# An encoder block: turned rows in another tile, the row blocks in another order

## The chip, the cores and the metric

The kernel runs on one core of one Trainium2 chip. A core has five engines that run side by side: TensorE (PE in the profile) multiplies matrices, VectorE (DVE) and ScalarE (ACT) work on rows of elements, GpSimd (POOL) does so too, and SyncE (SP) issues transfers. Each engine takes its instructions in the order of the program; semaphores make one wait for another. The metric is the device time of one execution in microseconds; smaller is better. Times in the text are microseconds from the start of the span unless said otherwise.

## The reference

One layer of a hybrid encoder on 1024 tokens (a grid of 16 rows and 64 columns) with 1024 channels, all in float32.

```python
u = rms_norm(x, norm1_g)
proj = u @ w_in
q, k, v, cb, cc, ch, ga, gb = split(proj)        # 512 x 6, then 1024 x 2
q, k = rms_norm(q per head, q_norm_g), rms_norm(k per head, k_norm_g)
y_a = neighbourhood_attention(q, k, v, rpb) @ w_attn_branch
y_b = (cb * conv3(cc * ch)) @ w_conv_branch
m = sigmoid(ga) * y_a + sigmoid(gb) * y_b
x = x + m @ w_o
x = x + relu(rms_norm(x, norm2_g) @ w_mlp_in)**2 @ w_mlp_out
```

The attention has 8 heads of 64 channels; each token looks at a window of 8 rows and 16 columns of the grid. The gates ga and gb are the projections that matter below as "the gates".

## The kernel before

**Arithmetic.** A float32 matrix is split into a high and a low half, both float16, after scaling by a power of two; a product is then three passes on TensorE (high by high, high by low, low by high; `PASSES`, L453). The high half is a scaled copy (ScalarE), the low half is the scaled value minus the high half (VectorE). The scale of a weight matrix needs a bound over all of it: squares with an accumulated sum on ScalarE (L266), a short sum on VectorE (L270, L272), a matmul with a matrix of ones, one column wide, that sums over the partitions (L201), and a few one-column instructions on VectorE. Only then are the high (L306) and low halves (L297) made.

**Rows.** The 1024 tokens are eight row blocks of 128. Row block b is loaded into `xt[:, b]` (L366). `norm` (L436) is a generator with four steps: the sum of squares (ScalarE, L439), the reciprocal root on GpSimd (L420, L421), the high half (L445, or GpSimd at L443 for blocks listed in `BYPOOL`), the low half (VectorE, L447). `ln_step(b, n)` runs n of these steps. The halves lie in `u16`, which has four places, block b in place b % 4. `turn_row(b)` (L518) has SyncE issue a transposing DMA of both halves into the columns of block b in `UT` (`uT` in the profile), from which TensorE reads them.

**V first, in two ways.** While the other blocks are still on their way, V of row blocks 0 and 1 is formed in float32 without the norm: `native_turn` (L563) transposes the raw rows on TensorE and stores them, scaled by the norm's gain, as `xT`; `native` (L574) multiplies them with V's raw weights, in two halves of 256 columns; `v_post` (L584) applies the row's scale and splits the result into `VT` (`vT`), which holds V as eight blocks of 128 tokens with a high and a low half. Before the change `xT` is a float32 view of the columns of row blocks 0 and 1 in `UT`, so that the two blocks are turned last. The other six blocks are V units, `v_unit` (L522): 24 matmuls of float16 halves and a split of the result into `VT[:, b]`.

**Q and K.** Sixteen units of 24 matmuls follow, eight row blocks for Q and eight for K (L743), each with a norm over each head (`qk_vec`). Weights come through a pool of five raw tiles; `load_upto(n)` issues loads up to tile n as the places come free. Tiles 0 to 3 are V's, 4 to 7 Q's, then K's. The preparation of a weight matrix (`prep`, L255) is a generator in `bg`, advanced by `tick`; work on the vector engines is in `fg`, advanced by `step`. What a unit leaves to be done with its result is put into `late` and done after the next unit's matmuls are in the queue, or at `settle()`.

**The gates' sums.** The gates use a scheme with seven instead of eight products, for which sums of row blocks n and n + 4 are formed from the normed rows: `sforms` (L481) scales both rows in place (ScalarE, L489), makes four sums in place (GpSimd, L493), and splits the pair into halves (L498, L500) that are stored to DRAM. `SFORM` (L479) lists the steps as (number of units done, n, whether it is the split).

The order of all this is written out by hand (L607 to L694). TensorE's queue holds: the transposes and float32 products with small sums between them, V units 2 to 7, then Q. SyncE's queue holds the loads and the transposing DMAs in the order written.

Of the kernel before, what the change touches and what calls it, by code (L numbers as in the profile page):

```python
# [10 lines left out]
F32 = mybir.dt.float32  # L11
# [4 lines left out]
OP = mybir.AluOpType  # L16
# [36 lines left out]
def encoder_block(ctx: ExitStack, tc: tile.TileContext, x, weights, cols, gqk, rel, masks, out):  # L53
# [12 lines left out]
    def bank(tag):  # L66
        return psum.tile([128, 512], F32, name="ps_" + tag, tag=tag, bufs=banks[tag])
# [29 lines left out]
    def at(c, i, n=1):  # L97
        return slice(c.start + i, c.start + i + n)
# [138 lines left out]
    def load_upto(n):  # L237
        while loaded[0] < min(n - held[0], limit[0], len(loads)):
            ch, p = loads[loaded[0]]
            loaded[0] += 1  # L240
            t = rawp.tile([128, 1024], F32, name="raw")
            load_into(t[:, :ch.widths[p][0] * ch.widths[p][1]], ch, p)
            ch.raw.append(t)
# [121 lines left out]
    def load_x(b):  # L365
        SP.dma_start(xt[:, b], x[b * 128:(b + 1) * 128, :])  # L366
# [10 lines left out]
    load_x(1)  # L377
    load_x(2)
    load_upto(4)
    load_x(3)  # L380
    load_x(4)
    SP.dma_start(gq.rearrange("p a d -> p (a d)"), bass.AP(tensor=gqk.tensor, offset=gqk.offset,
                                                           ap=[[0, 128], [1, 2 * HD]]))
    idi = w1p.tile([128, 128], I32, name="idi", bufs=1)
# [51 lines left out]
    def norm(xin, sq, u, y, pool):  # L436

        ss = tmp()
        A.activation(sq, xin, AF.Square, accum_out=sc[:, ss])  # L439
        yield  # L440
        yield from rpow(ss, D, y, 9)
        if pool:
            G.tensor_scalar(u[:, 0], xin, sc[:, y], 1.0, op0=OP.mult, op1=OP.mult)  # L443
        else:
            A.activation(u[:, 0], xin, AF.Copy, scale=sc[:, y])  # L445
        yield
        V.scalar_tensor_tensor(u[:, 1], xin, sc[:, y], u[:, 0], op0=OP.mult, op1=OP.subtract)  # L447

    def ln_turn(u16, b, dst):
        SP.dma_start_transpose(dst[:, :, :, b * 128:(b + 1) * 128].rearrange("p s k t -> p (s k) t"),  # L450
                               u16.rearrange("p s k -> p (s k)"))
# [19 lines left out]
    sgq, isgq = keep(), keep()  # L471
    sq = w1p.tile([128, D], F32, name="sq", bufs=1)
    ys = keep(8)
    BYPOOL = ()
    ln = [norm(xt[:, b], sq, u16[:, b % 4], at(ys, b), b in BYPOOL) for b in range(8)]
    GS = dram.tile([128, 4, 4, 2, 512], F16, name="gs")

    turned, formed = set(), [0]
    SFORM = ((7, 2, 0), (7, 3, 0), (8, 0, 0), (9, 1, 0), (9, 2, 1), (10, 3, 1), (11, 0, 1), (12, 1, 1))  # L479

    def sforms():  # L481

        for mark, n, split in SFORM:
            yield from apart(mark, 0)
            pair = xt[:, n:n + 5:4]
            if not split:
                assert n in turned and n + 4 in turned
                for b in (n, n + 4):
                    A.activation(xt[:, b], xt[:, b], AF.Copy, scale=sc[:, at(ys, b)])  # L489
                z = [xt[:, b, c:c + 512] for b in (n, n + 4) for c in (0, 512)]  # L490
                for o, a, b, op in ((3, 2, 3, OP.subtract), (2, 0, 2, OP.subtract),
                                    (0, 3, 0, OP.subtract), (1, 1, 0, OP.add)):
                    G.tensor_tensor(z[o], z[a], z[b], op=op)  # L493
                continue
            v = wqk.tile([128, 4, 2, 512], F16, name="s16", bufs=3)
            v4 = v.rearrange("p (b h) w c -> p b h w c", b=2)
            f = pair.rearrange("p b (h c) -> p b h c", h=2)
            A.activation(v4[:, :, :, 0], f, AF.Copy)  # L498
            yield
            V.tensor_tensor(v4[:, :, :, 1], f, v4[:, :, :, 0], op=OP.subtract)  # L500
            fg.append(sform_store(n, v))
# [6 lines left out]
    def ln_step(b, n=1):  # L508
        for _ in range(n):
            advance(ln[b])  # L510
# [5 lines left out]
        yield from gain(g, 11, sgq, isgq)  # L516

    def turn_row(b):  # L518
        ln_turn(u16[:, b % 4], b, UT)
        turned.add(b)  # L520

    def v_unit(b, ticks):  # L522
        ps = bank("ds"[b % 2])
        order = [(k, p) for k in range(8) for p in PASSES]
        if b == 2:
            order.sort(key=lambda o: o[1] == HL)

        def post():
            hi, lo = (VT[:, b, s] for s in range(2))
            A.activation(hi, ps, AF.Copy, scale=2.0 ** -20)  # L530
            V.scalar_tensor_tensor(lo, ps, 2.0 ** -20, hi, op0=OP.mult, op1=OP.subtract)
        unit(group(ps, [(UT[:, sa, k, b * 128:(b + 1) * 128], vhome[0][:, :, sw, k * 256:(k + 1) * 256])
                        for k, (sa, sw) in order]), post, 0, ticks)
# [8 lines left out]
    def v_scale(ch, floor, power):  # L542
        V.tensor_scalar(sc[:, ch.b], ch.sum[:, 0:1], floor, None, op0=OP.max)
        for _ in power:
            pass
        V.tensor_scalar(sc[:, ch.rm], sc[:, g1], sc[:, ch.s], None, op0=OP.mult)
# [11 lines left out]
                    done[0] += 1  # L558

    vps, raised = {}, {}  # L560
    xT = [UT.bitcast(F32)[:, b, :, 0:128] for b in range(2)]

    def native_turn(b):  # L563

# [9 lines left out]
    def native(b, j, ks):  # L574

        if (b, j) not in vps:
            vps[b, j] = bank("ds"[b])
        for k in ks:
            T.matmul(vps[b, j][:, :256], xT[b][:, k], cV[j].raw[k // 4][:, k % 4 * 256:k % 4 * 256 + 256],
                     start=k == 0, stop=k == 7)  # L580
        if ks[-1] == 7:
            units[0] += 1
# [47 lines left out]
    native(0, 1, eight)  # L630
    ln_step(2)
    turn_row(2)
    ln_step(3, 2)
    v_part(v0, 1, lower)
    v_scale(v1, 1e-30, pow2(v1.b, 14, v1.s, v1.inv, False, v1.more))
    load_x(5)
    load_x(6)
    load_upto(5)
    v_part(v0, 0, upper)
    ln_step(3)  # L640
    ln_step(4, 2)
    native(1, 1, eight)
    ln_step(3)
    turn_row(3)
    v_part(v1, 0, eight)
    v_part(v0, 1, upper)
    load_x(7)
    load_upto(7)
    V.tensor_reduce(sc[:, gm2], sc[:, g1], axis=AX, op=OP.max, apply_absolute_value=True)
    mul(gm2, gm2, gm2)  # L650
    ln_step(4)
    v_part(v1, 1, eight)
    ln_step(4)
    turn_row(4)
    load_upto(8)
    push(cQ)
    for b in 0, 1, 5:
        ln_step(b, 2)
    for j in range(2):
        for b in range(2):  # L660
            v_post(b, j, 0)
    ln_step(5)
    v_unit(2, 0)
    ln_step(5)
    turn_row(5)
    load_upto(done[0] + 5)
    for j in range(2):
        for b in range(2):
            v_post(b, j, 1)
    ln_step(6, 3)  # L670
    v_unit(3, 0)
    ln_step(6)
    turn_row(6)
    ln_step(7, 3)
    tick(2)
    ln_step(7)
    turn_row(7)
    fg.append(qk_gain())
    fg.append(sforms())
    ln_step(0)  # L680
    tick(2)
    ln_step(0)
    turn_row(0)
    step(2)
    for b in range(4, 8):
        v_unit(b, 8)
        step(2)
        if b == 4:
            ln_step(1)
        if b == 5:  # L690
            ln_step(1)
            turn_row(1)
    settle()
    flush()  # L694

# [35 lines left out]
        res.append(t)  # L731

    q16 = {}
    todo = [("q", b) for b in range(8)] + [("k", b) for b in range(8)]

    def finish_qk(n):
        kind, b = todo[n]
# [4 lines left out]

    for n, (kind, b) in enumerate(todo):  # L743
        ch = cQ if kind == "q" else cK
        if b == 0:
            push(cK if kind == "q" else cConv[0])
        ps = bank("do"[n % 2])
        q16[n] = []

        def post(ps=ps, kind=kind, n=n, ch=ch):  # L750
            fg.append(qk_vec(ps, ch.inv, kind, q16[n]))
        unit(tok_mms(ps, actU, b, ch, 8, 512, 0), post, 4, 6 if 4 < n < 8 else 3)
        if n == 3:
            forced[0] = True
            while formed[0] < 4:
                step()
            forced[0] = False
            QD = base.tile([128, 4, 2, 2, S], F16, name="qD", tag="Q")
            KD = base.tile([128, 8, S], F16, name="kD", tag="K")
            pln.close()  # L760
            base2 = ctx.enter_context(tc.tile_pool(name="base2", bufs=1))
            BT = base2.tile([128, 2, 4, S], F16, name="bT", tag="B")
            pbias = ExitStack()
            wbias = pbias.enter_context(tc.tile_pool(name="pbias", bufs=2, reuse_waits="tile"))
            mk = wbias.tile([128, 2, 384], BF16, name="mk", bufs=1)
            SP.dma_start(mk, masks)
            cneg, cinv = keep(), keep()
            V.tensor_scalar(sc[:, cneg], sc[:, isgq], -(2.0 ** -15), None, op0=OP.mult)
            V.tensor_scalar(sc[:, cinv], sc[:, sgq], 2.0 ** 15, None, op0=OP.mult)
            bias = {0: bias_load(0)}  # L770
        if n >= 3:
            finish_qk(n - 3)
        if n in (5, 6):
            bias_make(*bias[0], n - 5)
        if b == 7:
            flush()


# [1139 lines left out]
```

## Time and profile before

| what | value |
|---|---|
| median of 3 runs | 1212.31 us (1211.92 to 1212.68) |
| the profiled execution, its own time | 1212.94 us |
| its span, first to last instruction | 1211.2 us |
| mean granted TensorE clock | 0.997 |
| ScalarE, VectorE, GpSimd busy | 63%, 77%, 36% of the span |

A line of the timeline has the start, the length, the engine, the line of the kernel, the operation, the tiles written and read, the shape and the number of instructions; the bracket gives the idle time before it and what ended it. A line of the windows has the stretch, its length, then the busy time of PE, PEld, DVE, ACT and POOL (each with the number of instructions), the granted clock as a share of full speed, the share of the DMA engines and GB/s. `SPq` marks what SyncE's queue did: a length there is the time to issue a transfer, not to finish it.

### The profile page before, as it was taken

Reading aid. Unit: us, or ns where it says so; the run is one execution under the profiler, and the core shown is the slowest. Engines: PE = TensorE matmul, PEld = TensorE weight load, DVE = VectorE, ACT = ScalarE, POOL = GpSimd, SP = SyncE. Lnnn points to the kernel's source line nnn. Section 1 sums busy time; section 2 is a strip of 40 time slices with the busy share of each in tenths; the row PEclk is TensorE's granted clock in tenths of the full one; section 3 lists DMA queues with packets and bytes.
Section 4 is the critical chain, followed back from the end, with each engine's and each line's share of the span. In section 5 each row is a group of like instructions: output and inputs, shape, how many; then the busy total and the mean of one; then the engine's idle time right before and its main releaser. Section 6 shows DMA issues by size and latency. Waiting matters only on the chain.

```text
span 1211.2 us, 16879 instructions
## 1 busy us (share of the span) xinstructions
PE 1192.5 (98%) x6206; PEld 575.5 (48%) x6206; DVE 937.3 (77%) x1721; ACT 766.0 (63%) x1187; POOL 431.2 (36%) x290
## 2 busy tenths in 40 slices
PE   7999999999999999999999999999999999999998
PEld 5444445555444444444458444444444444444444
DVE  6597888998468686887888655455449999999997
ACT  7876678878445545436769777677776754646440
POOL 2441003231411111101004565665557471564562
PEclk8999999999999999999999999999999999999999
DMA  6967466666552121126196555355375825335302
GB/s 229 203 229 156 90 155 110 144 137 120 118 131 70 36 70 55 55 78 231 27 174 166 174 191 188 127 164 187 127 269 200 343 100 203 145 124 206 105 35 104
DMA packets 177250, 174.91 MB, mean 144 GB/s; under 512 B 137744, under 2 KB 138256, under 8 KB 173072
## 3 DMA queue, kind: packets, MB, share of 16 engines
q1 hardware_dynamic: 176592, 169.65, 48.7%
q10 hardware_dynamic: 576, 4.19, 0.8%
q8 instruction: 48, 0.79, 0.3%
q14 instruction: 34, 0.28, 0.1%
HBM read 102.51 MB, written 37.75 MB: 116 GB/s over the span
## 4 chain that ended last, share of the span: by engine, by line
PE 78%; DVE 4%; SPq 1%; issue 1%; ACT 1%; DMA 0%; DVEq 0%; ACTq 0%
PE ps_d L210 28%; PE ps_s L210 24%; PE ps_o L210 17%; PE ps_d L1013 7%; PE ps_o L990 1%; PE ps_s L933 1%; SPq L1084 1%; DVE w_s L1137 1%; DVE P L973 1%; DVE sg L1253 0%; DVE sz L947 0%; DMA uT<-gs 0%; ACT w_s L1141 0%; DVE sc L317 0%; DVE m L1255 0%
## 5 line engine op out<-in xcount | busy, mean ns | idle before, releaser
L210 PEld LDWEIGHTS <-ops 128*128 128x128 f16 x1356 | 132.5, 98 | 157.3
L210 PEld LDWEIGHTS <-w 128*128 128x128 f16 x1368 | 132.8, 98 | 139.5
L1013 PE MATMUL ps_d<-uT,w_ws 128*128 128x512 f16 x528 | 123.7, 379 | 0.1
L210 PE MATMUL ps_d<-ops 128*128 128x512 f16 (+1 forms) x528 | 118.3, 374 | 0.0
L1739 ACT ACTIVATE ops<-hf,sc 128x2048 f16<-128x2048 f32 x26 | 52.0, 2000 | 97.4 <-PE ps_o L210 34.9
L210 PE MATMUL ps_s<-ops 128*128 128x512 f16 x492 | 112.9, 379 | 0.0
L1126 POOL TENSOR_TENSOR tsum<-raw 128x512 f32<-128x512 f32 x28 | 46.2, 1663 | 148.9 <-ACT raw L1112 148.8
L1319 POOL TENSOR_TENSOR as<-as 128x512 f32<-128x512 f32 x56 | 77.5, 1385 | 38.5 <-ACT as L1599 35.2
L210 PEld LDWEIGHTS <-w_s 128*128 128x128 f16 x588 | 56.7, 98 | 70.2 <-DVE w_s L1137 1.8
L210 PEld LDWEIGHTS <-uT 128*128 128x128 f16 x528 | 51.3, 98 | 66.9 <-issue 3.9
L210 PE MATMUL ps_d<-u2x,w 128*128 128x512 f16 (+1 forms) x360 | 80.0, 372 | 0.0
L1741 DVE SCALAR_TENSOR_TENSOR ops<-hf,sc,ops 128x2048 f16<-128x2048 f32 x26 | 74.3, 2858 | 4.5 <-ACT ops L1739 4.5
L210 PE MATMUL ps_o<-ops 128*128 128x512 f16 x336 | 77.1, 379 | 0.0
L1013 PEld LDWEIGHTS <-w_ws 128*128 128x128 f16 x528 | 51.1, 98 | 54.5 <-DVE cv L835 0.3
L1112 ACT ACTIVATE raw<-raw,sc 128x256 f32<-128x256 f32 x172 | 71.1, 493 | 1.3 <-DMA raw<-in_weights 1.3
L210 PE MATMUL ps_o<-u2T,w 128*128 128x512 f16 (+1 forms) x324 | 71.7, 371 | 0.0
L1126 POOL TENSOR_TENSOR gsum<-raw 128x512 f32<-128x512 f32 x14 | 19.0, 1376 | 132.6 <-issue 71.3
L1141 ACT ACTIVATE w<-raw,sc 128x512 f16<-128x512 f32 (+1 forms) x28 | 24.6, 927 | 54.1 <-DVE sc L432 54.1
L297 DVE SCALAR_TENSOR_TENSOR w_ws<-raw,sc,w_ws 128x512 f16<-128x512 f32 (+2 forms) x72 | 51.1, 763 | 4.7 <-ACT w_ws L306 4.7
L210 PE MATMUL ps_s<-u2T,w 128*128 128x512 f16 (+1 forms) x252 | 52.7, 359 | 0.0
L1632 DVE TENSOR_TENSOR as<-ps_d,as 128x512 f32<-128x512 f32 (+1 forms) x14 | 9.4, 672 | 55.8 <-ACT as L1651 53.4
L956 ACT ACTIVATE sz<-sz,sc 128x384 f32<-128x384 f32 (+1 forms) x64 | 37.2, 581 | 22.4 <-DVE sc L947 15.0
(359 smaller groups left out, 2631.3 us busy)
## 6 DMA issues: line engine op xcount, KB each, us to landing
raw<-in_weights SPq DMA_DIRECT2D x88, 512.0 KB, 5.6
hs<-as SPq DMA_DIRECT2D x16, 1792.0 KB, 8.7
hf<-hs SPq DMA_DIRECT2D x26, 1024.0 KB, 7.5
w2x<-in_weights SPq DMA_DIRECT2D x16, 512.0 KB, 8.5
raw<-in_weights SPq DMA_DIRECT2D x16, 384.0 KB, 3.4
xt<-in_x SPq DMA_DIRECT2D x8, 512.0 KB, 5.5
gs<-s ACTq DMA_DIRECT2D x4, 1024.0 KB, 4.3
x<-in_x SPq DMA_DIRECT2D x8, 512.0 KB, 10.2
```

The source lines that it names most:

```text
L210: T.matmul(ps, l, r, start=a, stop=b)
L297: V.scalar_tensor_tensor(lo, self.raw[p][:, o:o + m], sc[:, c:c + 1], hi, op0=OP.mult, op1=OP.subtract)
L933: T.matmul(ps[:, :nb * 128], QD[:, p, e, w, i * 128:(i + 1) * 128], KD[:, 2 * p + e, lo * 128:(lo + nb) * 128], start=w == 0, stop=w == 1)
L956: A.activation(z, z, AF.Exp, scale=-1.0, bias=sc[:, d["mx"]], accum_out=sc[:, d["sm"]])
L973: V.scalar_tensor_tensor(d["lo"], d["z"][:, :d["n"]], sc[:, d["r"]], d["hi"], op0=OP.mult, op1=OP.subtract)
L1013: T.matmul(ps, l, r, start=a, stop=b)
L1112: A.activation(v, v, AF.Copy, scale=sc[:, at(g, 4 * i + k)])
L1126: G.tensor_tensor(t[:, o], a, b, op=OP.add)
L1141: A.activation(o(0), w, AF.Copy, scale=sc[:, s])
L1319: sub.tensor_tensor(z[o], z[a], z[b], op=op)
L1739: A.activation(P[:, 1, 0], hf, AF.Copy, scale=sc[:, Rs])
L1741: V.scalar_tensor_tensor(P[:, 1, 1], hf, sc[:, Rs], P[:, 1, 0], op0=OP.mult, op1=OP.subtract)
```

## The change

The turned float32 rows `xT` are kept in blocks 4 to 7 of `VT`, two blocks for each row block, instead of in `UT`. The row blocks are taken in the order 2, 6, 3, 7, 4, 5, 0, 1 (`ORDER`) for the norm, V and Q; places in `u16` and the PSUM banks of V's units follow it. The loads of x, the norm's steps and the weight loads are written out anew in that order. The high halves of blocks 3, 7, 4 and 5 are made by GpSimd (`BYPOOL`). `sforms` is cut into `sform_rows` and `sform_sums`, and the row scalings and sums of the pairs (2, 6) and (3, 7) are issued between V's units, after its first and third one; those of the pairs 0 and 1 stay in `sforms` with new marks. The steps of Q's weight preparation begin behind V's first unit, and its matmul with the ones stands behind V's third unit. All results of the float32 products, high and low, are split before the first V unit.

```diff
@@ -377,8 +377,8 @@
     load_x(1)
     load_x(2)
     load_upto(4)
+    load_x(6)
     load_x(3)
-    load_x(4)
     SP.dma_start(gq.rearrange("p a d -> p (a d)"), bass.AP(tensor=gqk.tensor, offset=gqk.offset,
                                                            ap=[[0, 128], [1, 2 * HD]]))
     idi = w1p.tile([128, 128], I32, name="idi", bufs=1)
@@ -471,12 +471,23 @@
     sgq, isgq = keep(), keep()
     sq = w1p.tile([128, D], F32, name="sq", bufs=1)
     ys = keep(8)
-    BYPOOL = ()
-    ln = [norm(xt[:, b], sq, u16[:, b % 4], at(ys, b), b in BYPOOL) for b in range(8)]
+    ORDER, BYPOOL = (2, 6, 3, 7, 4, 5, 0, 1), (3, 7, 4, 5)
+    ln = [norm(xt[:, b], sq, u16[:, ORDER.index(b) % 4], at(ys, b), b in BYPOOL) for b in range(8)]
     GS = dram.tile([128, 4, 4, 2, 512], F16, name="gs")
 
     turned, formed = set(), [0]
-    SFORM = ((7, 2, 0), (7, 3, 0), (8, 0, 0), (9, 1, 0), (9, 2, 1), (10, 3, 1), (11, 0, 1), (12, 1, 1))
+    SFORM = ((9, 0, 0), (9, 2, 1), (10, 1, 0), (10, 3, 1), (11, 0, 1), (12, 1, 1))
+
+    def sform_rows(n):
+        assert n in turned and n + 4 in turned
+        for b in (n, n + 4):
+            A.activation(xt[:, b], xt[:, b], AF.Copy, scale=sc[:, at(ys, b)])
+
+    def sform_sums(n):
+        z = [xt[:, b, c:c + 512] for b in (n, n + 4) for c in (0, 512)]
+        for o, a, b, op in ((3, 2, 3, OP.subtract), (2, 0, 2, OP.subtract),
+                            (0, 3, 0, OP.subtract), (1, 1, 0, OP.add)):
+            G.tensor_tensor(z[o], z[a], z[b], op=op)
 
     def sforms():
 
@@ -484,13 +495,8 @@
             yield from apart(mark, 0)
             pair = xt[:, n:n + 5:4]
             if not split:
-                assert n in turned and n + 4 in turned
-                for b in (n, n + 4):
-                    A.activation(xt[:, b], xt[:, b], AF.Copy, scale=sc[:, at(ys, b)])
-                z = [xt[:, b, c:c + 512] for b in (n, n + 4) for c in (0, 512)]
-                for o, a, b, op in ((3, 2, 3, OP.subtract), (2, 0, 2, OP.subtract),
-                                    (0, 3, 0, OP.subtract), (1, 1, 0, OP.add)):
-                    G.tensor_tensor(z[o], z[a], z[b], op=op)
+                sform_rows(n)
+                sform_sums(n)
                 continue
             v = wqk.tile([128, 4, 2, 512], F16, name="s16", bufs=3)
             v4 = v.rearrange("p (b h) w c -> p b h w c", b=2)
@@ -516,11 +522,11 @@
         yield from gain(g, 11, sgq, isgq)
 
     def turn_row(b):
-        ln_turn(u16[:, b % 4], b, UT)
+        ln_turn(u16[:, ORDER.index(b) % 4], b, UT)
         turned.add(b)
 
     def v_unit(b, ticks):
-        ps = bank("ds"[b % 2])
+        ps = bank("ds"[ORDER.index(b) % 2])
         order = [(k, p) for k in range(8) for p in PASSES]
         if b == 2:
             order.sort(key=lambda o: o[1] == HL)
@@ -558,7 +564,8 @@
                     done[0] += 1
 
     vps, raised = {}, {}
-    xT = [UT.bitcast(F32)[:, b, :, 0:128] for b in range(2)]
+    xT = [VT[:, 4 + 2 * b:6 + 2 * b].rearrange("p r w c -> p (r w c)").bitcast(F32).rearrange("p (k t) -> p k t", k=8)
+          for b in range(2)]
 
     def native_turn(b):
 
@@ -630,66 +637,73 @@
     native(0, 1, eight)
     ln_step(2)
     turn_row(2)
-    ln_step(3, 2)
+    load_x(7)
+    load_x(4)
+    load_upto(5)
+    ln_step(6, 2)
     v_part(v0, 1, lower)
     v_scale(v1, 1e-30, pow2(v1.b, 14, v1.s, v1.inv, False, v1.more))
+    v_part(v0, 0, upper)
+    ln_step(6)
+    ln_step(3, 2)
+    native(1, 1, eight)
+    ln_step(6)
+    turn_row(6)
     load_x(5)
-    load_x(6)
-    load_upto(5)
-    v_part(v0, 0, upper)
+    v_part(v1, 0, eight)
+    v_part(v0, 1, upper)
+    load_upto(7)
     ln_step(3)
-    ln_step(4, 2)
-    native(1, 1, eight)
+    V.tensor_reduce(sc[:, gm2], sc[:, g1], axis=AX, op=OP.max, apply_absolute_value=True)
+    mul(gm2, gm2, gm2)
+    v_part(v1, 1, lower)
+    load_upto(8)
+    v_part(v1, 1, upper)
     ln_step(3)
     turn_row(3)
-    v_part(v1, 0, eight)
-    v_part(v0, 1, upper)
-    load_x(7)
-    load_upto(7)
-    V.tensor_reduce(sc[:, gm2], sc[:, g1], axis=AX, op=OP.max, apply_absolute_value=True)
-    mul(gm2, gm2, gm2)
-    ln_step(4)
-    v_part(v1, 1, eight)
+    push(cQ)
+    ln_step(7, 3)
+    ln_step(0, 2)
+    ln_step(1, 2)
+    ln_step(7)
+    turn_row(7)
+    for s in range(2):
+        for j in range(2):
+            for b in range(2):
+                v_post(b, j, s)
+    ln_step(4, 3)
+    ln_step(5, 3)
+    v_unit(2, 0)
+    settle()
     ln_step(4)
     turn_row(4)
-    load_upto(8)
-    push(cQ)
-    for b in 0, 1, 5:
-        ln_step(b, 2)
-    for j in range(2):
-        for b in range(2):
-            v_post(b, j, 0)
-    ln_step(5)
-    v_unit(2, 0)
+    load_upto(done[0] + 5)
     ln_step(5)
     turn_row(5)
-    load_upto(done[0] + 5)
-    for j in range(2):
-        for b in range(2):
-            v_post(b, j, 1)
-    ln_step(6, 3)
+    sform_rows(2)
+    sform_sums(2)
+    tick(2)
+    v_unit(6, 0)
+    settle()
+    tick(3)
     v_unit(3, 0)
-    ln_step(6)
-    turn_row(6)
-    ln_step(7, 3)
-    tick(2)
-    ln_step(7)
-    turn_row(7)
+    sform_rows(3)
+    sform_sums(3)
+    tick()
+    v_unit(7, 6)
+    ln_step(0)
     fg.append(qk_gain())
     fg.append(sforms())
-    ln_step(0)
     tick(2)
     ln_step(0)
     turn_row(0)
-    step(2)
-    for b in range(4, 8):
+    for b in 4, 5:
         v_unit(b, 8)
-        step(2)
         if b == 4:
             ln_step(1)
-        if b == 5:
             ln_step(1)
             turn_row(1)
+        step(3)
     settle()
     flush()
 
@@ -731,7 +745,7 @@
         res.append(t)
 
     q16 = {}
-    todo = [("q", b) for b in range(8)] + [("k", b) for b in range(8)]
+    todo = [("q", b) for b in ORDER] + [("k", b) for b in range(8)]
 
     def finish_qk(n):
         kind, b = todo[n]
@@ -742,7 +756,7 @@
 
     for n, (kind, b) in enumerate(todo):
         ch = cQ if kind == "q" else cK
-        if b == 0:
+        if n % 8 == 0:
             push(cK if kind == "q" else cConv[0])
         ps = bank("do"[n % 2])
         q16[n] = []
@@ -772,7 +786,7 @@
             finish_qk(n - 3)
         if n in (5, 6):
             bias_make(*bias[0], n - 5)
-        if b == 7:
+        if n % 8 == 7:
             flush()
```

## The prediction

> **What bounds the kernel now.** I read the page's busy shares first, then the busy time by windows of 10 us, then TensorE's timeline between 15 and 77 us, and last what SyncE's queue waited for.
>
> ```profile
> PE 1192.5 (98%) x6206; PEld 575.5 (48%) x6206; DVE 937.3 (77%) x1721; ACT 766.0 (63%) x1187; POOL 431.2 (36%) x290
> ...
> 20.00:30.00 10.00, 6.23 (x15) 5.04 (x16) 6.90 (x20) 8.74 (x18) 4.13 (x8) 0.66 0.77 213
> 40.00:50.00 10.00, 8.60 (x41) 3.73 (x40) 4.06 (x9) 9.78 (x15) 1.43 (x2) 1.00 1.08 249
> 60.00:70.00 10.00, 8.12 (x37) 3.40 (x36) 10.00 (x7) 10.00 (x10) 9.69 (x7) 1.00 0.63 168
> ```
>
> TensorE is busy for 98% of the span, so a change that leaves the matmuls alone can win only where TensorE stands still or runs slowly. Apart from the first five microseconds these windows hold nearly all such places. The timeline gives them one by one (start, length, instructions; in brackets the idle time before and what ended it).
>
> ```profile
> 15.62 3.70 PE L579 MATMUL ps_d<-raw,uT 128*128 128x256 f32 x16
> 18.72 0.59 PE L579 MATMUL ps_d<-raw,uT 128*128 128x256 f32 x2
> 23.77 6.64 PE L579 MATMUL ps_s<-raw,uT 128*128 128x256 f32 x16 [4.45 <-DMA uT<-u]
> 30.24 5.34 PE L210 MATMUL ps_d<-w_v,uT 128*128 128x512 f16 x24
> 35.42 5.34 PE L210 MATMUL ps_s<-w_v,uT 128*128 128x512 f16 x24
> 42.17 5.35 PE L210 MATMUL ps_d<-w_v,uT 128*128 128x512 f16 x24 [1.40 <-DMA uT<-u]
> 62.92 3.92 PE L210 MATMUL ps_d<-w_ws,uT 128*128 128x512 f16 x16
> 67.72 0.81 PE L210 MATMUL ps_d<-w_ws,uT 128*128 128x512 f16 x3 [0.87 <-DVE w_ws L297]
> 71.50 5.34 PE L210 MATMUL ps_o<-w_ws,uT 128*128 128x512 f16 x24
> ```
>
> The float32 product of rows 0 and 1 with V's second half ends with row block 0 at 18.72 + 0.59 = 19.31; the same sixteen matmuls for block 1 begin only at 23.77, behind a transposing DMA into uT, and take 6.64 where their like took 3.70. A V unit of 24 matmuls then advances TensorE by 35.42 - 30.24 = 5.18. So three sums are lost: 30.24 - 19.32 - 3.70 = 7.22 around the second product, 42.17 - 35.42 - 5.18 = 1.57 before the third V unit, and 71.50 - 62.92 - 5.17 = 3.41 in Q's first unit, which waits three times for its low weight halves. Together 12.20 us. The slow product has the clock as its cause (last figures before the DMA share: the granted clock):
>
> ```profile
> 22.00:23.00 1.00, 0.00 (x0) 0.00 (x0) 1.00 (x4) 1.00 (x3) 0.00 (x0) 0.94 1.16 211
> 23.00:24.00 1.00, 0.23 (x1) 0.23 (x2) 1.00 (x4) 1.00 (x2) 0.00 (x0) 0.50 1.12 106
> 29.00:30.00 1.00, 1.00 (x4) 0.84 (x3) 0.00 (x0) 0.18 (x1) 0.00 (x0) 0.64 0.06 16
> ```
>
> It fell to half some 3.6 us after TensorE stopped and came back only when 6 us of matmuls had run; the waits of 1.40 and 0.87 left it at 1.00.
>
> **The change, part by part.** *The turned rows in V's tile.* Today they lie in uT, and SyncE's queue shows the price:
>
> ```profile
> SPq L450 <- PE ps_s L579: 7.0, 1, 7.0
> SPq L450 <- PE ps_d L579: 3.3, 1, 3.3
> ```
>
> The transpose of row block 2 stood 3.3 us, and that of 3 stood 7.0 us, until float32 products had read uT; the product of block 1 in turn waited for block 2's transpose. The columns do not overlap, so it is the shared tile that couples them. With the rows in blocks 4 to 7 of vT, which nothing writes until a V unit for such a block has ended, the second product follows at 19.32 and ends at 23.0, at full clock. The first V unit needs block 2's transpose and V's high halves; it starts at 23.0 instead of 30.24. This removes the whole 7.22.
>
> *The transposes and loads on SyncE.* What now comes late is data:
>
> ```profile
> 19.35 1.97 SPq L450 DMA_TRANSPOSE uT<-u  x1
> 30.44 1.98 SPq L450 DMA_TRANSPOSE uT<-u  x1
> 32.47 0.94 SPq L366 DMA_DIRECT2D xt<-in_x  x1
> 33.45 0.92 SPq L234 DMA_DIRECT2D raw<-in_weights  x2
> 34.46 5.58 SPq L450 DMA_TRANSPOSE uT<-u  x1
> ...
> uT<-u SPq DMA_TRANSPOSE x1, 4.2
> ...
> uT<-u SPq DMA_TRANSPOSE x1, 7.7
> ```
>
> The last two rows are the times to landing of the transposes issued at 30.44 and 34.46: 4.2 with a free queue, 7.7 behind three loads, so a load costs (7.7 - 4.2) / 3 = 1.17. After the change block 2's transpose is issued when its low half is done, at about 16.05 (the row at 14.72 below plus 1.28), and lands near 20.4. Rows 7 and 4 and a weight tile follow, then block 6: the same pattern as 30.44 to 34.46, so it lands 42.16 - 30.44 = 11.7 after block 2's issue, at 27.8. The first V unit ends at 28.2: in time by 0.4. Behind block 6, whose issue holds the queue till 25.7 as the 5.58 did, stand rows 5 and three weight tiles (0.46 each to issue), then block 3, issued at about 27.7. It lands between 27.8 + 4 x 1.17 + 2.6 = 35.1, if the loads stream right behind block 6 (2.6 is the 4.2 without what overlaps), and 27.7 + 4.2 + 4 x 1.17 = 36.6. I take 35.8. The second V unit ends at 33.4, so the third waits 2.4. Blocks 7, 4 and 5 follow with no or one load between them and are wanted at 42, 48 and 53: hidden behind V units.
>
> *Q's scale now stands ahead of the fourth V unit.* Its one-column matmul is put into TensorE's queue between V units three and four; before, between four and five of the six. It needs the squares of all four of Q's tiles, which ScalarE does in order behind much else:
>
> ```profile
> 14.72 1.28 DVE L447 SCALAR_TENSOR_TENSOR u<-xt,sc,u 128x1024 f16<-128x1024 f32 x1
> 19.88 3.29 ACT L554 ACTIVATE w_v<-raw,sc 128x256 f16<-128x256 f32 x8
> 22.01 3.25 DVE L556 SCALAR_TENSOR_TENSOR w_v<-raw,sc,w_v 128x256 f16<-128x256 f32 x8
> 24.11 1.04 ACT L439 ACTIVATE sq<-xt 128x1024 f32<-128x1024 f32 x1
> 25.27 1.06 ACT L439 ACTIVATE sq<-xt 128x1024 f32<-128x1024 f32 x1
> 28.34 0.47 ACT L590 ACTIVATE vT<-ps_s,sc 128x256 f16<-128x256 f32 x1 [0.38 <-DVE sc L588]
> 45.77 0.58 ACT L530 ACTIVATE vT<-ps_s 128x512 f16<-128x512 f32 x1
> 54.12 2.05 DVE L447 SCALAR_TENSOR_TENSOR u<-xt,sc,u 128x1024 f16<-128x1024 f32 x1
> 55.23 2.17 ACT L489 ACTIVATE xt<-xt,sc 128x1024 f32<-128x1024 f32 x2
> ...
> L1755 POOL TENSOR_TENSOR raw<-raw 128x1024 f32<-128x1024 f32 x8 | 30.8, 3866 | 36.4 <-DVE ops L1750 36.4
> L867 POOL TENSOR_SCALAR cv<-cv,sc 128x1024 f32<-128x1024 f32 x4 | 4.5, 1122 | 42.2 <-DVE sc L102 16.3 <-DVE sc L433 16.0 <-ACT sz L956 10.0
> ```
>
> ScalarE is through with V's high halves at 23.2; the squares of rows 7, 0 and 1 (1.16 apart) end at 26.7. Then it stands before the first scaled V result, whose scale comes from VectorE, in order behind V's low halves (22.01 + 3.25 = 25.3) and the low halves of blocks 3 and 7. Their high halves are now GpSimd's: no row has such an instruction writing float16, so its price lies between L867 (1.12, same operation and size) and L1755 (3.87, two inputs); I take 1.12 to 1.6, since it is the same operation. VectorE's own price is 1.28 alone and 2.05 beside a busy GpSimd (the row at 54.12). That makes the scale ready between 28.0 (25.3 + 2 x 1.28 + 0.16) and 30.7 (with one blocked stretch of 1.1 and 2 x 2.05); I take 29.5. From there: four scaled results 1.9, two squares 2.3, V's block 2 0.6, rows 2 and 6 scaled 2.2, two of Q's squares 2.4, V's block 6 0.6, two more squares 2.4: 41.9, and 0.6 for two short VectorE steps. The matmul runs near 42.5 (41.2 to 44), the fourth V unit starts at 42.7. Without either wait that would be 23.0 + 3 x 5.18 = 38.5, so 4.2 us are lost again, 2.4 for block 3 and 1.8 here.
>
> The Trainium skill (SBUF — State Buffer, Who interferes with whom) says that a VectorE instruction with two SBUF inputs and a GpSimd one that reads SBUF exclude each other for a whole instruction. It speaks against moving high halves to GpSimd; by it the scale would come at the late bound, and the fourth unit at 43.9, 1.2 us of the gain. The pair 1.28 and 2.05 agrees in kind.
>
> *The gates' sums.* Eight GpSimd sums move forward, to about 37 to 51, and ScalarE's four row scalings with them.
>
> ```profile
> 48.50 26.93 POOL L493 TENSOR_TENSOR xt<-xt 128x512 f32<-128x512 f32 x16 [9.46 <-ACT xt L489]
> 58.52 12.49 DVE L297 SCALAR_TENSOR_TENSOR w_ws<-raw,sc,w_ws 128x512 f16<-128x512 f32 x8
> ```
>
> Sixteen sums in a row (1.68 each) covered all of Q's low halves, 1.56 each; that is the 3.41 lost. After the change the first low half starts near 47.5. Even if all eight were slowed, with block 0's low half (2.05) and a V result among them, they end at 62.8, and Q's first unit, from 58.3, asks for the last tile after 18 of its 24 matmuls, at 62.2. I price this at 0 (0.6 at most); the cover is the last two V units, without which 3.4 is back. Later stages are the same instructions in another row order, and VectorE's and ScalarE's work between the V and Q units is done some ten us earlier, ahead of TensorE's eight; I cost them at nothing.
>
> *Sum.* 12.20 removed, 2.4 + 1.8 put back: 8.0 us. The profiled run of before took 1212.94 (span 1211.2), which makes 1204.9; against the median of 1212.31 it is **1204.3**. A measurement of this kernel can tell about 0.2%, 2.4 us.
>
> **The rivals.** *No new waits* (block 3 lands by 33.4, the squares by 38): 1212.3 - 12.2 = 1200.1. For it: the queues drain faster than I allow; against: four loads ahead of block 3.
>
> *The clock halves.* If block 3 is in time, the whole 4.2 falls into one wait for Q's scale, longer than the 3.6 after which the clock fell at 23; the fourth unit then pays up to 6.64 - 3.70 = 2.9 more: 1207.2. Against: two waits with a V unit between them stay below. The Trainium skill (TensorE: Matmul & The Clock Gate, Part 1) puts the window at about 3.4 us, free-running, so that a wait even of 4 us may or may not halve it. The trace's 3.6 agrees.
>
> *The tile does not matter.* If the transposes' waits came with something other than the shared tile, the 7.22 stays and only part of the 5.0 behind it goes: about 1209.5. Against: both waits end exactly with L579.
>
> *Slower: GpSimd's high halves.* At L1755's 3.87 each, four of them in the chain, block 7's low half comes at 31.5 and, through blocks 4 and 5 (whose low halves stand ahead of Q's sum on VectorE), the scale at 48: the fourth unit loses 9.7 and, the wait being 7, 2.9 more for the clock: 12.6 against 12.2 won. It decides from a scale at 47.4; at 4.6 a half the time is about 1214.9. Against it: the 1.12 of L867.
>
> **How the numbers follow.** Forecast 0.47, clock 0.22, no new waits 0.12, tile 0.10, slower 0.09. The range reaches from just above the second-best case, 1200.5, to 1208.8, which takes in the half clock together with a scale at its late bound. Faster by more than 0.2%: 0.47 + 0.22 + 0.12 + half of the tile's case, 0.86; within: 0.07; slower: 0.07.
>
> **What would show it.** Right: the second float32 product begins at 19.3 and takes 3.7; V's first unit begins at 23; a wait before the third unit that ends with a DMA into uT, and one before the fourth that ends with VectorE's sum; no wait for L297 in Q's first unit; Q's second unit begins near 63.5. Wrong: a clock of 0.50 after 23 us; a GpSimd high half above 2 us; block 6 landing after 28.2; or new waits behind Q.

## The result, and the profile after

The changed kernel takes 1206.54 us (median of 6 runs, 1205.77 to 1207.31) against 1212.12 (6 runs, 1210.96 to 1212.75) for the kernel before beside it: a ratio of 0.9955, 95% interval 0.9942 to 0.9968. That is 5.6 us less, where 8.0 were forecast. The profiled execution took 1206.38, with a span of 1204.6; between the two profiled executions lie 6.6 us.

TensorE is now busy for 99% of the span. Two windows of 10 us of the changed kernel (stretch, length, busy time of PE, PEld, DVE, ACT, POOL, granted clock, DMA share, GB/s):

```profile
20.00:30.00 10.00, 8.13 (x38) 4.61 (x36) 8.59 (x18) 6.68 (x16) 7.61 (x8) 1.00 1.09 260
30.00:40.00 10.00, 7.05 (x32) 3.07 (x33) 5.36 (x11) 9.30 (x17) 6.77 (x10) 1.00 1.10 265
```

TensorE still loses 4.8 us between 20 and 40, and no clock is lost. Two small gaps are new between 140 and 160, where the windows show TensorE busy for 9.57 of 10 us. TensorE's timeline names all four:

```profile
19.33 3.62 PE L586 MATMUL ps_s<-raw,vT 128*128 128x256 f32 x16
22.79 5.34 PE L210 MATMUL ps_d<-w_v,uT 128*128 128x512 f16 x24
30.20 5.35 PE L210 MATMUL ps_s<-w_v,uT 128*128 128x512 f16 x24 [2.07 <-DMA uT<-u]
38.30 5.36 PE L210 MATMUL ps_d<-w_v,uT 128*128 128x512 f16 x24 [2.75 <-DMA uT<-u]
43.49 0.17 PE L201 MATMUL ps_o<-ones 128*128 128x1 bf16 x1
43.52 5.34 PE L210 MATMUL ps_s<-w_v,uT 128*128 128x512 f16 x24
...
59.06 5.34 PE L210 MATMUL ps_d<-w_ws,uT 128*128 128x512 f16 x24
64.24 5.34 PE L210 MATMUL ps_o<-w_ws,uT 128*128 128x512 f16 x24
...
147.76 5.34 PE L210 MATMUL ps_o<-uT,w_ws 128*128 128x512 f16 x24 [0.43 <-ACT qs L724]
153.53 0.16 PE L201 MATMUL ps_d<-ones 128*128 128x1 bf16 x1 [0.43 <-DVE ones L272]
```

The second float32 product now runs straight behind the first, at full clock, and V's first unit starts at 22.79 instead of 30.24. Two waits for uT are there, before V's second and third unit. The matmul for Q's scale (43.49) has no wait of its own: V's third unit ends then, and the value it needs was ready at 43.37, 0.1 us before. Q's first unit has no wait either. Q's second unit starts 71.50 - 64.24 = 7.26 us earlier than before. The two late waits, at the end of K, are 0.86 us together against 0.16 at the same place before; they take 0.7 back. The remaining difference to 5.6 is in which executions were profiled: before's was 0.8 above the median of its six runs, after's 0.2 below.

SyncE's queue and GpSimd's high halves (L443, of blocks 3, 7, 4 and 5 in turn), from the changed kernel's timeline:

```profile
16.20 1.95 SPq L450 DMA_TRANSPOSE uT<-u  x1
...
20.45 5.54 SPq L450 DMA_TRANSPOSE uT<-u  x1
21.32 1.58 POOL L443 TENSOR_SCALAR u<-xt,sc 128x1024 f16<-128x1024 f32 x1
25.79 2.38 POOL L443 TENSOR_SCALAR u<-xt,sc 128x1024 f16<-128x1024 f32 x1
26.03 1.24 SPq L366 DMA_DIRECT2D xt<-in_x  x1
...
28.79 11.93 SPq L450 DMA_TRANSPOSE uT<-u  x3
34.36 1.12 POOL L443 TENSOR_SCALAR u<-xt,sc 128x1024 f16<-128x1024 f32 x1
```

The transpose of block 2 no longer waits for a product (16.20 instead of 19.35). Block 6 is issued at 20.45, 4.25 us behind block 2 where the pattern of the forecast had 4.02, yet V's second unit gets it only at 30.20; block 3 is issued at 28.79, a microsecond later than forecast. The fourth GpSimd half took 1.12 us like the third.

### The profile page after: what moved, and what is told of

It reads as the page before. It is cut to its first block, busy times and chain, and to the rows that moved or that the text cites. A ratio compares the mean times of both kernels' runs of the same rounds, so it can differ in the third digit from the quotient of the medians.

```text
span 1204.6 us, 16885 instructions
## 1 busy us (share of the span) xinstructions
PE 1189.3 (99%) x6206; PEld 573.4 (48%) x6206; DVE 933.8 (78%) x1721; ACT 761.4 (63%) x1183; POOL 441.2 (37%) x294
## 4 chain that ended last, share of the span: by engine, by line
PE 77%; DVE 5%; issue 1%; SPq 1%; ACT 1%; DMA 0%; DVEq 0%; ACTq 0%
PE ps_d L210 27%; PE ps_s L210 24%; PE ps_o L210 17%; PE ps_d L1027 7%; PE ps_o L1004 1%; PE ps_s L947 1%; SPq L1098 1%; DVE w_s L1151 1%; DVE P L987 1%; DVE ops L1764 1%; DVE sg L1267 0%; DVE sz L961 0%; DVE x L1863 0%; ACT w_s L1155 0%; DMA uT<-gs 0%
## 5 line engine op out<-in xcount | busy, mean ns | idle before, releaser
L297 DVE SCALAR_TENSOR_TENSOR w_ws<-raw,sc,w_ws 128x512 f16<-128x512 f32 (+2 forms) x72 | 45.4, 683 | 5.5 <-ACT w_ws L306 5.5
```

What stands on the lines that cost most here:

```text
L297: V.scalar_tensor_tensor(lo, self.raw[p][:, o:o + m], sc[:, c:c + 1], hi, op0=OP.mult, op1=OP.subtract)
```

## Experiments

Eleven kernels; each ratio is to the kernel before, measured beside it, with its 95% interval. It is the estimate on record and need not be the quotient of the two medians. The kernels were measured on several chips, so two of them are compared by their ratios and not by their medians alone.

| run | median us | ratio |
|---|---|---|
| tile_back | 1211.55 | 0.9992 (0.9983 to 1.0001) |
| tile_alone | 1210.22 | 0.9982 (0.9973 to 0.9992) |
| no_gpsimd_halves | 1212.77 | 1.0007 (0.9997 to 1.0016) |
| sums_late | 1213.86 | 1.0015 (1.0006 to 1.0024) |
| loads_behind | 1209.12 | 0.9975 (0.9966 to 0.9985) |
| scale_behind_4th | 1209.28 | 0.9977 (0.9967 to 0.9987) |
| loads_and_scale | 1206.57 | 0.9955 (0.9942 to 0.9969) |
| pairs_behind | 1207.86 | 0.9957 (0.9945 to 0.9969) |
| all_three | 1206.07 | 0.9947 (0.9935 to 0.9959) |
| k_sooner | 1212.73 | 1.0005 (0.9996 to 1.0014) |
| k_sooner_pairs | 1203.35 | 0.9937 (0.9923 to 0.9950) |

### The parts of the change, one at a time

**The tile undone.**

```diff
-    xT = [VT[:, 4 + 2 * b:6 + 2 * b].rearrange(...).bitcast(F32).rearrange(...) for b in range(2)]
+    xT = [UT.bitcast(F32)[:, b, :, 0:128] for b in range(2)]
```

> The changed kernel with the turned float32 rows put back into uT; order, GpSimd halves, sums and Q's preparation as changed. Theory (the shared tile made the transposes wait): the transpose of block 2 waits for the first float32 product again (issue near 19.5 instead of 16.2), the second product starts near 24 instead of 19.3 at half clock, V's first unit near 30 instead of 22.8. Of these 7 us part is a wait that the changed kernel has anyway (4.8 us before its second and third V unit), so Q's second unit moves from 64.2 to 69 or 70 and the time is 1210.5 to 1212.5. Rival (the order of the blocks did it, not the tile): 1206 to 1207.

TensorE's timeline of this run:

```profile
24.70 5.26 PE L585 MATMUL ps_s<-raw,uT 128*128 128x256 f32 x16 [4.50 <-DMA uT<-u]
29.80 5.34 PE L210 MATMUL ps_d<-w_v,uT 128*128 128x512 f16 x24
...
42.70 5.35 PE L210 MATMUL ps_d<-w_v,uT 128*128 128x512 f16 x24 [2.38 <-DMA uT<-u]
...
63.45 2.75 PE L210 MATMUL ps_d<-w_ws,uT 128*128 128x512 f16 x12
```

And two lines of what SyncE's queue waited for (in total, times, longest):

```profile
SPq L450 <- PE ps_s L585: 5.6, 1, 5.6
...
SPq L450 <- PE ps_d L585: 3.5, 1, 3.5
```

The transposes wait for the float32 products again, and the wait of 4.5 us and the slow product are back. It is the shared tile that made the transposes wait; the rival falls, and without the tile the rest of the change is worth nothing measurable (0.9983 to 1.0001). The 7 us cost 4.4 at Q's start (63.45 against 59.06), since one of the later waits is then covered. The profiled execution (1209.70) is one of the shortest of the ten.

**The tile alone**, in the kernel before:

```diff
-    xT = [UT.bitcast(F32)[:, b, :, 0:128] for b in range(2)]
+    xT = [VT[:, 4 + 2 * b:6 + 2 * b].rearrange(...).bitcast(F32).rearrange(...) for b in range(2)]
```

> The kernel of before with only the turned rows moved into vT. Theory: the second product at 19.3 with full clock and V's first unit near 23, a gain of 7.2 us at that place; block 3's transpose stands behind three loads as block 6's does in the changed kernel, so a wait of 1 to 2 us before the second unit is put back and one before the third; Q's first unit still waits 2 to 3.4 us for its low halves beside the gates' sums. Time 1206 to 1209. Rival (the tile is worth nothing without the order): 1211.5 to 1212.5.

V's first two units and the start of Q's first in the timeline, then a line of TensorE's waits (in total, times, longest):

```profile
22.54 5.34 PE L210 MATMUL ps_d<-w_v,uT 128*128 128x512 f16 x24
29.07 5.35 PE L210 MATMUL ps_s<-w_v,uT 128*128 128x512 f16 x24 [1.19 <-DMA uT<-u]
...
56.96 1.03 PE L210 MATMUL ps_d<-w_ws,uT 128*128 128x512 f16 x4
```

```profile
PE ps_d L210 <- DVE w_ws L297: 5.7, 7, 0.9
```

Q begins at 56.96, two us before the changed kernel's, and then waits 5.7 us for its low halves. The time is 1.2 us above the range I gave: the waits in Q's first unit grew with TensorE's lead instead of staying at 3.4 or less. So the tile wins six us at Q's start, of which some two are left in the time; the rest of the change is there to keep them.

**GpSimd's high halves undone.**

```diff
-    ORDER, BYPOOL = (2, 6, 3, 7, 4, 5, 0, 1), (3, 7, 4, 5)
+    ORDER, BYPOOL = (2, 6, 3, 7, 4, 5, 0, 1), ()
```

> The changed kernel with the high halves of blocks 3, 7, 4 and 5 made by ScalarE again. Theory A (block 6's transpose lands late because GpSimd's high half and VectorE's low half run while it moves; in the changed kernel the data stood still from 26.4 to 27.5, inside that pair): the wait before the second V unit falls from 2.07 to below 1.0 us. Theory B (it lands late because of the three loads queued ahead of it): the wait stays between 1.8 and 2.3. In both ScalarE gets 4.5 us more and VectorE's low halves start earlier; Q's sum at 42.5 to 45; time 1205 to 1208.

```profile
30.62 5.35 PE L210 MATMUL ps_s<-w_v,uT 128*128 128x512 f16 x24 [2.32 <-DMA uT<-u]
...
48.38 0.16 PE L201 MATMUL ps_o<-ones 128*128 128x1 bf16 x1 [4.28 <-DVE ones L272]
48.40 8.08 PE L210 MATMUL ps_s<-w_v,uT 128*128 128x512 f16 x24
```

Theory A falls: block 6's wait is 2.32, and not shorter, with no GpSimd half near it. The time missed my range by almost 5 us, for I had Q's scale at 45 at the latest: the four halves cost ScalarE some 4.5 us, all of it ahead of Q's squares, the scale comes 4.9 us later, TensorE stands for 4.28 us, and the unit behind runs at half clock (8.08 for 5.34). Without the GpSimd halves nothing of the gain is left, just as without the tile: each of the two is needed.

**The gates' sums undone** (the split of the step into two functions stays):

```diff
-    SFORM = ((9, 0, 0), (9, 2, 1), ...
+    SFORM = ((9, 2, 0), (9, 3, 0), (9, 0, 0), (9, 2, 1), ...
...
-    sform_rows(2)
-    sform_sums(2)
...
-    sform_rows(3)
-    sform_sums(3)
```

> The changed kernel with the row scalings and the gates' sums of the pairs (2, 6) and (3, 7) put back behind V's units; Q's preparation as early as changed. Theory (the early preparation of Q removed the 3.4 us of waits in Q's first unit, not the early sums): no wait for Q's low halves, Q's second unit at 64.2 or up to 1 us earlier, and a later place gives back up to 2 us since the pairs' halves end later on VectorE: 1206 to 1208.5. Rival (the early sums removed them): the waits for Q's low halves return, 2 to 3.4 us, time 1208.5 to 1210.

TensorE's timeline, before V's second unit and at K's sum:

```profile
30.61 7.04 PE L210 MATMUL ps_s<-w_v,uT 128*128 128x512 f16 x24 [2.60 <-DMA uT<-u]
...
87.40 0.16 PE L201 MATMUL ps_s<-ones 128*128 128x1 bf16 x1 [2.36 <-DVE ones L272]
88.59 7.03 PE L210 MATMUL ps_o<-w_ws,uT 128*128 128x512 f16 x24 [1.03 <-ACT qs L720]
```

GpSimd's sums (L490), and one of ScalarE's high halves of a pair (L504), which waits for them:

```profile
55.06 27.17 POOL L490 TENSOR_TENSOR xt<-xt 128x512 f32<-128x512 f32 x16 [16.61 <-ACT xt L484]
```

```profile
75.05 1.91 ACT L504 ACTIVATE s<-xt 128x2048 f16<-128x2048 f32 x1 [4.80 <-POOL xt L490]
```

Q's first unit is free of waits, as the theory said, but 7 us are lost later, far outside my range. Sixteen sums in a row hold back the pairs' halves, these hold back Q's results on ScalarE, and TensorE meets the delay at K's sum (2.36), at a PSUM bank that a Q result still holds (1.03), and in the half clock behind; the rest goes in waits for K's halves and at the end of K. In this profile V's second unit lost the clock as well.

### Where the two waits for uT come from, and what stands behind them

**Fewer loads ahead of blocks 6 and 3.**

```diff
     load_x(7)
-    load_x(4)
-    load_upto(5)
...
     turn_row(6)
+    load_x(4)
     load_x(5)
...
-    load_upto(7)
...
-    load_upto(8)
...
     turn_row(3)
+    load_upto(6)
...
     turn_row(7)
+    load_upto(8)
```

> The changed kernel with the loads ahead of block 6's transpose cut from three to one and those ahead of block 3's from four to two; Q's tiles are loaded behind block 3's and block 7's transposes. Theory (the two waits for uT are the loads queued ahead): no wait before the second V unit (now 2.07) and below 1 us before the third (now 2.75); the third unit ends near 38.5 and Q's scale is ready as now, near 43.4, so the 4.8 us come back as one wait of 4 to 5 us ahead of the fourth unit, which then runs at half clock, 2 to 3 us more: 1207.5 to 1210. Rival (the queue does not matter, the transposes are slow themselves): both waits stay within 0.5 us and the time within 1205.5 to 1207.5.

```profile
27.97 5.34 PE L210 MATMUL ps_s<-w_v,uT 128*128 128x512 f16 x24
...
44.76 0.16 PE L201 MATMUL ps_o<-ones 128*128 128x1 bf16 x1 [6.27 <-DVE ones L272]
44.78 8.15 PE L210 MATMUL ps_s<-w_v,uT 128*128 128x512 f16 x24
```

Both waits are gone: the loads ahead made them. All of it returns as one wait of 6.27 for Q's scale, which comes 1.3 us later than in the changed kernel, and the next unit pays 2.8 for the half clock. The 1.3 come from the edit itself: two of Q's squares on ScalarE now wait 1.20 and 0.46 us for weight tiles whose loads it moved back. The other 5 us would have been lost anyway. So the two short waits of the changed kernel cost nothing in sum: they stand in for a longer one.

**Q's scale behind V's fourth unit**, alone and with the loads:

```diff
-    tick()
-    v_unit(7, 6)
+    v_unit(7, 7)
```

> The changed kernel with Q's one-column matmul behind V's fourth unit instead of ahead of it. It costs TensorE no wait now, so nothing is won; Q's low halves start 5 us later, near 53, and meet the sums of pair 0. Theory (the early scale is what removed the waits in Q's first unit): waits for Q's low halves of 2 to 5 us return, 1208.5 to 1211. Rival (the early sums alone keep Q's first unit free of waits): 1206 to 1207.

> Both edits together. V's six units then run with less than 1 us of waits from 22.8, Q's first unit starts near 54 to 55 instead of 59.1, with the low halves of Q as early as in the changed kernel (below 1 us of waits). Theory (behind Q's first unit TensorE waits for the vector engines and GpSimd, whose chain is not moved): most of the 4.5 us comes back as waits for Q's results, for K's sum or K's low halves between 75 and 160, and the time is 1204.5 to 1206.5. Rival (TensorE alone sets the end, so what is won in V stays): 1201.5 to 1203.

Alone, the edit leaves Q's first unit without a wait, so my theory fell; with the sums early, a scale 4.5 us later is early enough there. But the time is 2.7 us longer by the ratios, so the rival's time was not met either. The largest loss at the end of K is this wait for a PSUM bank:

```profile
149.02 5.34 PE L210 MATMUL ps_o<-uT,w_ws 128*128 128x512 f16 x24 [1.33 <-ACT qs L723]
```

Beside it stand 0.53 us for K's low halves and 1.3 instead of 0.3 us in later waits for the gates' rows.

Both edits together, ScalarE's timeline, then TensorE's:

```profile
67.47 1.91 ACT L504 ACTIVATE s<-xt 128x2048 f16<-128x2048 f32 x1 [4.45 <-POOL xt L490]
```

```profile
54.82 5.34 PE L210 MATMUL ps_d<-w_ws,uT 128*128 128x512 f16 x24
...
97.75 0.38 PE L210 MATMUL ps_d<-w_ws,uT 128*128 128x512 f16 x1 [1.04 <-ACT w_ws L306]
99.21 6.83 PE L210 MATMUL ps_d<-w_ws,uT 128*128 128x512 f16 x23 [1.09 <-DVE w_ws L297]
```

Q begins 4.2 us earlier than in the changed kernel and the time is the same. All 4.2 come back: 2.1 as waits for K's halves, the rest as half clock and at the end of K. So TensorE does not set the end here alone. The waits point to a chain over GpSimd's sums, the pairs' halves and Q's results on ScalarE and VectorE, in which ScalarE stood idle for 4.45 us; the next runs move it.

### Moving that chain

**The pairs' halves two units later**, in the changed kernel and with the two edits above:

```diff
-    SFORM = (..., (11, 0, 1), (12, 1, 1))
+    SFORM = (..., (13, 0, 1), (14, 1, 1))
```

> The changed kernel with the halves of pairs 0 and 1 taken two units later (marks 13 and 14 instead of 11 and 12), so that Q's first results stand ahead of them on ScalarE and VectorE. In the changed kernel ScalarE stood 4.45 us before a pair's half, waiting for GpSimd's sums. Theory (what was given back, 0.43 + 0.43 us between Q and the convolution, comes from that chain): V as in the changed kernel, Q's second unit at 64.2, the two waits of 0.43 gone or halved, 1205.5 to 1206.5. Rival (the chain is bound by the transposes of Q's results through SyncE): the same waits, 1206 to 1207.

> Loads behind, Q's scale behind V's fourth unit, and the halves of pairs 0 and 1 two units later. Theory (with both of the first edits Q begins 4.2 us sooner, and K's halves were late because ScalarE waited for GpSimd's sums ahead of Q's results): the waits of 1.04 and 1.09 us in K's first unit and the half clock behind them go, and 3 to 4 us stay: 1202 to 1204. Rival (ScalarE and VectorE are full between Q and the convolution whatever their order): waits return later and the time is 1205 to 1206.5.

In the first, one of the two late waits is gone. But the profiled execution lost the clock at V's third unit (6.74 behind a wait of 2.68), so that Q came 2 us later, and that alone may have covered the wait: in loads_behind, with the pairs where they were and Q later still, it is gone too. The runs spread from 1204.88 to 1209.53, so this run is inconclusive. In the second, whose profiled execution (1208.02) was the longest of five, K's first unit waits longer than in the two edits alone:

```profile
98.62 0.59 PE L210 MATMUL ps_d<-w_ws,uT 128*128 128x512 f16 x1 [2.80 <-ACT w_ws L306]
99.79 7.70 PE L210 MATMUL ps_d<-w_ws,uT 128*128 128x512 f16 x23 [0.58 <-DVE w_ws L297]
```

The pairs' halves only changed places with Q's first results; ScalarE's work ahead of K's high halves is the same, and they begin at 97.86 instead of 96.99. The median (1206.07) lies in the rival's range, though single runs went from 1204.91 to 1208.02.

**K's sum two units sooner**, on top of the two edits (loads and scale), without and with the pairs later:

```diff
-                yield from apart(units[0], 1 if self.kind == "Q" else 3)
+                yield from apart(units[0], 1 if self.kind in "QK" else 3)
```

> Loads behind and Q's scale behind V's fourth unit, and K's sum allowed one unit after its squares instead of three, so that K's halves stand about one Q unit (3.8 us) sooner on ScalarE and VectorE. Theory (of what V won, 4.2 us, the waits for K's halves took 2.1 and the half clock behind them 1.9; it is the place of K's halves in the queues, not a lack of ScalarE's and VectorE's time): no wait in K's first unit, no half clock, and 2 to 3.5 us less than the 1206.6 of the two edits alone: 1203 to 1204.6; some 1 us may come back at the end of K. Rival (the vector engines are full there): the time stays at 1206 to 1207, the waits come back as waits for the results' banks at the end of K.

> As the run beside it, with the halves of pairs 0 and 1 two units later as well. With K's halves a unit sooner the wait of 2.80 us in K's first unit and the half clock of its 7.70 us run go. Theory: 1202.5 to 1204.5. Rival (full engines): 1205.5 to 1206.5.

One line of TensorE's timeline for the first, two for the second:

```profile
79.95 0.16 PE L201 MATMUL ps_s<-ones 128*128 128x1 bf16 x1 [9.40 <-DVE ones L272]
```

```profile
71.58 0.16 PE L201 MATMUL ps_s<-ones 128*128 128x1 bf16 x1 [1.21 <-DVE ones L272]
...
144.59 5.34 PE L210 MATMUL ps_o<-uT,w_ws 128*128 128x512 f16 x24 [0.28 <-ACT qs L722]
```

Alone it is a bad trade: K's sum stands in TensorE's queue while K's last square waits on ScalarE behind a pair's half, and that behind GpSimd's sums: 9.40 us, a case that neither theory had. With the pairs out of the way the same matmul waits 1.21 us, K's first unit none, and the waits do not come back at the end of K (0.28 there, and 0.44 at the sum behind it), as they would have if the vector engines were full. So in this trace it was places in queues, not a lack of vector time. The median of 1203.35 is the lowest here, 3.2 us below the changed kernel's, but two of its five runs (1206.17 and 1206.66) lie among the changed kernel's, and the intervals of the two ratios overlap: by the ratios the gain is some 2 us, and it is likely rather than shown.

## Why the prediction was right, and where it was off

The forecast mechanism held, and 5.6 of the 8.0 us came. But the waits that take part of the gain back do not all stand where they were forecast, and three of the four signs of being wrong did appear: a GpSimd half above 2 us, block 6 landing after 28.2, and new waits behind Q. They cost little, for the reasons below.

- *The tile.* Right. The product was forecast at 19.3 and V's first unit at 23.0; measured 19.33 and 22.79. That the shared tile is the cause was shown by tile_back and tile_alone.
- *Block 6 lands at 27.8, in time by 0.4.* Wrong by 2.3 us; this step failed. I took the pattern of block 4 in the kernel before, 11.7 us from the issue of one transpose to the landing of the next; it was 30.2 - 16.2 = 14.0. That loads ahead make a transpose late is shown (loads_behind removes the wait). Why the same pattern took 2.3 us longer here is only in part known: some 1 us of it is a pause that the last section shows, the rest stays open.
- *Block 3 makes the third unit wait 2.4.* The place was right; that the size (2.75) came near was luck. Block 3 was there at 38.30, 2.5 us after the forecast of 35.8 and above its bound of 36.6. The wait is no longer because the second unit had slid by 2.1 us as well.
- *Q's scale at 42.5, the fourth unit at 42.7.* The matmul ran at 43.49, the unit at 43.52. This term is why the sum held: loads_behind shows that with block 6 and block 3 in time the scale alone holds the fourth unit there, so the wrong landings changed where TensorE stood and hardly how long. ScalarE's work ended at 42.01, against 41.9 forecast. Missing were 0.8 us behind it: the two short VectorE steps, put at 0.6, took 1.4. The second one took 1.14 us here, while GpSimd's sums ran (from 38.52 to 50.29); in sums_late, with no sums at that time, it took 0.16. Beside the sums it varied from run to run (0.20 in tile_back, 1.08 in no_gpsimd_halves). One line of VectorE's timeline for each, the changed kernel's first:

```profile
42.23 1.14 DVE L272 TENSOR_TENSOR ones<-sc 128x1 bf16<-128x1 f32 x1
```

```profile
40.73 0.16 DVE L272 TENSOR_TENSOR ones<-sc 128x1 bf16<-128x1 f32 x1
```

- *GpSimd's halves at 1.12 to 1.6.* They took 1.58, 2.38, 1.12 and 1.12. The 2.38 is above the bound, beside VectorE's low half; TensorE did not wait for it, since V's third unit ended after the scale was ready. What I left unsaid is their worth: without them 6 us, shown by no_gpsimd_halves.
- *The clock.* No loss, as in the forecast. The rival's mechanism is real: where TensorE stood 4.28 and 6.27 us for the scale, the unit behind took 8.08 and 8.15 instead of 5.34. But waits as short as those of the changed kernel did lose the clock in other runs (last section), so that it kept the clock is in part luck.
- *Q's first unit without waits.* Right. My reason, the early preparation, is not the whole one: with a scale one unit later and early sums (scale_behind_4th), and with late sums and the early scale (sums_late), it is free of waits too. Either of the two was enough there.
- *Later stages at nothing.* Off by 0.7 us. What the two late waits come from was not shown. What sums_late did show, and I did not see, is that "ahead of TensorE's eight" holds only as long as the sums are early; when they are not, 7 us return near K.
- *Sum.* V's first unit came 0.2 us sooner than forecast, 1.0 us more was lost between it and the fourth unit (5.2 against 4.2), and 0.7 at the end of K: 8.0 + 0.2 - 1.0 - 0.7 = 6.5, beside 6.6 in the span. The medians show 5.6, for the reason given with the result.

## What to carry to other kernels

Two tensors that share a tile can make transfers wait that have nothing to do with each other; look for a transfer whose release is a matmul that reads other columns. A gain ahead of a chain on other engines is only worth what that chain can follow: before pricing the work behind it at nothing, ask which engine's queue the first late result stands in. And short waits can be worth keeping: closing both of them here (loads_behind) made one long wait and cost some 2.5 us, and closing them together with that long wait won nothing; the lowest median came only when the work behind was moved as well.

## What was not expected of the hardware

**The clock can fall after waits well below 3.6 us.** It halved behind a wait of 2.60 (sums_late), in one of 2.68 that followed one of 1.80 (pairs_behind), and behind 1.04 and 1.09 with one matmul in between (loads_and_scale), but not behind 2.07 and 2.75 in the changed kernel. The 3.6 us of the prediction is thus no threshold. In sums_late the clock fell only after TensorE had started again; windows of 1 us:

```profile
30.00:31.00 1.00, 0.39 (x2) 0.21 (x3) 0.25 (x5) 0.47 (x1) 0.64 (x2) 1.00 0.99 369
31.00:32.00 1.00, 1.00 (x6) 0.43 (x4) 0.93 (x4) 0.99 (x3) 0.00 (x0) 0.75 1.08 430
32.00:33.00 1.00, 1.00 (x4) 0.35 (x3) 0.78 (x2) 1.00 (x2) 0.00 (x0) 0.50 0.99 393
```

Nor does it fall a fixed time after TensorE stops. In pairs_behind TensorE stopped at 36.2, and the clock fell near 38.3, 2.1 us later; in loads_behind it stopped at 38.5, and the clock fell near 43.7, 5.2 us later. The half microsecond of each fall, pairs_behind first:

```profile
38.00:38.50 0.50, 0.00 (x0) 0.00 (x0) 0.00 (x0) 0.50 (x2) 0.40 (x2) 0.80 1.28 284
```

```profile
43.50:44.00 0.50, 0.00 (x0) 0.00 (x0) 0.17 (x2) 0.50 (x3) 0.50 (x1) 0.67 2.91 228
```

The Trainium skill (TensorE: Matmul & The Clock Gate, Part 1) has a throttle after an idle window of about 3.4 us; by these rows a wait of 2.6 can be enough. Part of the spread between runs of one kernel may come from this: in k_sooner_pairs the three runs with a mean clock of 0.999 or 1.000 took 1202.43 to 1203.35, the two with 0.998 took 1206.17 and 1206.66. In pairs_behind the clock does not explain it (1204.88 at 0.998, 1208.88 at 1.000).

**Transfers stood still behind a transpose.** In the changed kernel almost no data moved between 26.5 and 27.5 (the DMA view of the two half microseconds), while SyncE took 1.24 us to issue the load behind block 6's transpose; the median of its eight loads of x is 0.51.

```profile
DMA packets 4, 0.00 MB, mean 2 GB/s; under 512 B 4, under 2 KB 4, under 8 KB 4
...
DMA packets 18, 0.00 MB, mean 9 GB/s; under 512 B 18, under 2 KB 18, under 8 KB 18
```

The windows of no_gpsimd_halves, tile_alone, pairs_behind and loads_behind have a pause of about 1 us too, each time when the load behind their second transpose is issued. The kernel before has no such pause where its block 4, the pattern of the forecast, was landing: between 38.0 and 41.5 its slowest half microsecond moved 151 GB/s. So the pause is, by its length, some 1 us of the 2.3 by which block 6 was late. What makes it was not tried and stays open.
